# Loading the first input tile in two transfers, of 16 and of 112 partitions

## The chip, the cores and the metric

The kernel runs on one core of one Trainium2 chip. The metric is the device time of one execution in microseconds (us). The kernel before was run three times: median 630.27 us, from 630.23 to 630.30 us.

## What is computed

```python
B, S, D = 8, 2048, 4096
x: float32 [8, 2048, 4096]      # 268 MB
w: float32 [4096, 1]

proj = (x @ w).squeeze(-1)                       # one dot product of 4096 per row of x
cm = np.maximum.accumulate(proj, axis=1)         # running maximum along S
is_record = (proj >= cm).astype(np.float32)
return np.cumsum(is_record, axis=1)              # running count of records, [8, 2048]
```

Nearly all of the data is x, and each of its elements is used once.

## The kernel before, in words

The rows of x are taken in groups along S. Three groups have four rows to a partition (512 rows of S each) and a fourth has three (384 rows); within a group there is one tile for each of the eight batches. A tile therefore has 128 partitions with 64 KB each (48 KB in the fourth group), and it is 8.39 MB. What is left of S, 128 rows of each batch, is the tail: eight tiles of 16 KB to a partition, the last two of them loaded in column pieces (list `TILES`).

All loads of x are issued by the SyncE queue (SP in the profile), in the order in which they are used: first the loop over groups `g` and tiles `t` (L165 to L176), then the tail (L194 to L205). There are three large buffers (`xbuf`, chosen by `at(g, t)`), so the first three loads have no wait, and each later one waits until the work on the tile that had its buffer is done (`user_before` and `free`, on the semaphores `fr` and `p7`). Each load adds 16 to a semaphore of its tile position, `xs[t]`, and the engines that read the tile wait for `xs[t]` to reach 16. The TensorE program takes these 16 off again after each group.

The work on a tile is split by columns. VectorE multiplies and sums columns 0 to 2815 of each row in one instruction (`dot`, L124, called from `group_dots`). GpSimd multiplies the other 1280 columns (`group_products`, L276), and ScalarE sums those products (`add_up`, L130). After a group, TensorE transposes the sums into PSUM (L312), and VectorE makes the running maximum, the comparison and the running count (`group_scans`). For the first three groups each engine's program is a hardware loop (`Fori`), whose first iteration serves the first tile too.

While the first tile loads, w is brought in by a small transfer from the ScalarE queue (L178), spread over the partitions by TensorE (L224) and copied by ScalarE (L231 to L235).

The issuing loop at the place of the change reads:

```python
i = SY.dma_start(
    out=at(g, t)[:, : r * D],
    in_=x[B - 1 - t, STARTS[g] : STARTS[g] + r * P, :].rearrange("(p r) d -> p (r d)", r=r),
).then_inc(xs[t], 16)
u, n = user_before(g, t)
if n:
    i._wait_ge(*(free(u, n)))
```

## Time and profile before

| | |
|---|---|
| Median of 3 runs | 630.27 us |
| Time of the profiled execution | 631.05 us |
| Span of its instructions in the profile | 629.3 us |
| Between the two | 1.75 us |
| Bytes read from HBM | 268.45 MB |
| VectorE (DVE) busy | 407.3 us, 65% |
| GpSimd (POOL) busy | 370.7 us, 59% |
| ScalarE (ACT) busy | 181.2 us, 29% |
| TensorE (PE) busy | 29.1 us, 5% |
| Queue of the SP loads | 98.9% of what 16 DMA engines' span holds |

All times inside the profile are counted from the start of the span. A load appears twice in it: as an instruction on the SP queue, which only hands it over, and as packets that the 16 DMA engines move, whose end is the landing. A packet of a large tile is one partition's row of 64 KB.

### The profile page before, as it was taken

What the parts mean: (1) busy time and instruction counts of PE and PEld (TensorE: products, weight loads), DVE (VectorE), ACT (ScalarE), POOL (GpSimd) and SP (SyncE); (2) the same over time, 40 slices, a digit from 0 to 9 for tenths busy, and PEclk for the clock granted to TensorE, in tenths of its full rate; (3) what the DMA queues carried; (4) which work ended last, traced back from release to release, by engine and by line L of the source; (5) the groups of instructions that cost most, each with busy time, mean ns of one, the idle gap of its engine ahead of it and who ended that gap; (6) DMA issues with size and microseconds to landing.
All of it is one profiled execution on the core that took longest, in us unless ns stands there. A gap on an engine that the chain in (4) does not pass through costs nothing. (4 is left out here: it accounts for less than half of the span.)

```text
span 629.3 us, 1140 instructions
## 1 busy us (share of the span) xinstructions
PE 29.1 (5%) x96; PEld 13.5 (2%) x96; DVE 407.3 (65%) x294; ACT 181.2 (29%) x274; POOL 370.7 (59%) x149
## 2 busy tenths in 40 slices
PE   8000000000020000000001000000002000000100
PEld 3000000000010000000000000000001000000000
DVE  0755775556766567755578655676556976655897
ACT  1222332223322233222233222332223232232254
POOL 0554675456765557745577555676557666555775
PEclk9999999999999999999996555555555555555565
DMA  9999999999999999999999999999999999999996
GB/s 401 400 467 400 446 421 425 442 437 429 442 425 450 417 450 417 459 408 458 408 458 408 458 408 458 408 459 408 462 418 438 416 447 441 413 447 444 404 425 248
DMA packets 6563, 268.54 MB, mean 427 GB/s; under 512 B 760, under 2 KB 1016, under 8 KB 1568
## 3 DMA queue, kind: packets, MB, share of 16 engines
q1 hardware_dynamic: 6544, 268.50, 98.9%
q10 hardware_dynamic: 16, 0.02, 0.0%
q14 instruction: 3, 0.02, 0.0%
HBM read 268.45 MB, written 0.07 MB: 427 GB/s over the span
## 5 line engine op out<-in xcount | busy, mean ns | idle before, releaser
L124 DVE CUSTOM_DVE_ANT_0 xall<-xall,w_v 128x2816 f32<-128x2816 f32 (+1 forms) x129 | 385.5, 3041 | 181.8 <-DMA xall<-in_x_dram 181.8
L276 POOL TENSOR_TENSOR xall<-xall,w_sb 128x1280 f32<-128x1280 f32 x120 | 345.0, 2909 | 246.7 <-DMA xall<-in_x_dram 243.3
L130 ACT ACTIVATE xall<-xall 128x1280 f32<-128x1280 f32 (+2 forms) x130 | 162.9, 1253 | 428.6 <-POOL xall L276 408.3
L312 PE MATMUL ps<-identity,small 128*8 128x128 f32 x60 | 13.0, 406 | 568.6 <-PEq L309 568.6
L130 ACT ACTIVATION_READ_ACCUMULATOR xall<-xall 128x1 f32 x130 | 24.2, 186 | 0.0
L336 POOL TENSOR_TENSOR xall<-xall,w_sb 128x1280 f32<-128x1280 f32 (+2 forms) x8 | 21.1, 2632 | 3.1 <-DMA xall<-in_x_dram 3.0
L312 PEld LDWEIGHTS ps<-identity,small 128*8 128x8 f32 x60 | 7.3, 125 | 575.4 <-issue 571.3
L140 DVE TENSOR_TENSOR_SCAN cm<-ps,cm,small 8x512 f32<-8x512 f32 (+3 forms) x8 | 7.0, 869 | 18.8 <-PE ps L312 18.4
L224 PE MATMUL w_v<-w,identity 8*128 8x512 f32 x14 | 12.1, 1056 | 0.0
L124 DVE DVE_READ_ACCUMULATOR2_ANT small<- 128x1 f32 x133 | 10.8, 81 | 0.0
L246 DVE MEMSET ps<- 8x512 f32 x1 | 0.5, 485 | 15.7 <-ACT w L235 15.7
L146 DVE TENSOR_TENSOR_SCAN cnt<-ps,cnt,small 8x512 f32<-8x512 f32 (+3 forms) x8 | 7.0, 870 | 0.3
L224 PEld LDWEIGHTS w_v<-w,identity 8*128 8x128 f32 x14 | 4.6, 332 | 7.3 <-issue 7.3
L143 DVE TENSOR_TENSOR ps<-ps,cm 8x512 f32<-8x512 f32 (+3 forms) x8 | 3.9, 487 | 0.3
L232 ACT COPY w_sb<-w_v 128x768 f32<-128x768 f32 x1 | 0.8, 799 | 11.4 <-PE w_v L224 11.4
L347 POOL TENSOR_TENSOR masked<-fold,small 128x4 f32<-128x4 f32 x8 | 1.6, 201 | 3.2 <-DVE small L124 3.2
L124 DVE CUSTOM_DVE_ANT_0 xall<-xall,w_v,small 128x480 f32<-128x480 f32 (+2 forms) x4 | 3.1, 810 | 0.2 <-DVE small L124 0.2
L357 PE MATMUL ps<-fold,masked 128*8 128x32 f32 x20 | 2.0, 235 | 25.3 <-ACT masked L352 17.7
L352 ACT ACTIVATE masked<-fold,small 128x4 f32<-128x4 f32 x10 | 3.0, 298 | 0.3
L336 POOL TENSOR_TENSOR xall<-xall,w 128x640 f32<-128x640 f32 (+1 forms) x2 | 2.3, 1137 | 0.1
L224 PE MATMUL ps<-w,identity 8*128 8x512 f32 x2 | 2.1, 1135 | 2.6 <-DMA w<-in_w_dram 2.6
L231 ACT ACT_TABLE_LOAD x1 | 1.3, 1283 | 2.7 <-DVE fold L242 2.7
(18 smaller groups left out, 5.3 us busy)
## 6 DMA issues: line engine op xcount, KB each, us to landing
xall<-in_x_dram SPq DMA_DIRECT2D x8, 6144.0 KB, 33.5
xall<-in_x_dram SPq DMA_DIRECT2D x6, 2048.0 KB, 42.4
xall<-in_x_dram SPq DMA_DIRECT2D x1, 1264.0 KB, 36.6
xall<-in_x_dram SPq DMA_DIRECT2D x1, 816.0 KB, 39.3
xall<-in_x_dram SPq DMA_DIRECT2D x1, 784.0 KB, 37.9
xall<-in_x_dram SPq DMA_DIRECT2D x2, 240.0 KB, 26.6
xall<-in_x_dram SPq DMA_DIRECT2D x1, 416.0 KB, 39.4
xall<-in_x_dram SPq DMA_DIRECT2D x24, 45.0
```

What stands on the lines that cost most here:

```text
L124: return V.tensor_tensor_reduce(out=xsl, in0=xsl, in1=wsl, scale=1.0, scalar=seed, op0=ALU.mult, op1=ALU.add, accum_out=dst,)
L130: return A.activation(out=xsl, in_=xsl, func=ACTF.Copy, accum_out=dst)
L140: V.tensor_tensor_scan(out=cm_, data0=src, data1=low, initial=cm0, op0=ALU.max, op1=ALU.max,)._wait_ge(psr, base).then_inc(psr, 1)
L143: V.tensor_tensor(out=src, in0=src, in1=cm_, op=ALU.is_ge)._wait_ge(psr, base + 1).then_inc(psr, 1)
L146: V.tensor_tensor_scan(out=cnt_, data0=src, data1=low, initial=cnt0, op0=ALU.add, op1=ALU.max,)._wait_ge(psr, base + 2).then_inc(cs, 1)
L224: i = T.matmul(out=dst, lhsT=identity[:NW, k : k + 1].to_broadcast([NW, P]), rhs=w_row, start=True, stop=True,).then_inc(bw, 1)
L276: i = G.tensor_mul(out=xl, in0=xl, in1=w_sb).then_inc(pl, 1)
L312: i = T.matmul(out=ps[:B, j : r * P : r], lhsT=l[:, j * B : (j + 1) * B], rhs=identity, start=k == 0, stop=k == 1,)
L336: G.tensor_mul(out=xl, in0=xl, in1=w_pool(*p))._wait_ge(xq[i], 16).then_inc(pl, 1)
L347: return eng.tensor_tensor(out=e, in0=by_b, in1=acc.to_broadcast([P, H]), op=ALU.mult)
L352: return A.activation(out=e, in_=by_b, func=ACTF.Copy, scale=acc)._wait_ge(pa, na).then_inc(ms, 1)
L357: return T.matmul(out=ps[:B, k * Q : (k + 1) * Q], lhsT=masked[:, n * B : (n + 1) * B], rhs=by_i, start=start, stop=stop,)
```

## The change

The load of tile `g == t == 0`, and no other, is issued as two instructions: the first has partitions 0 to 15 and adds 16 to a new semaphore, `xf`; the second has partitions 16 to 127 and adds 16 to `xs[0]` as before. VectorE and GpSimd each get one wait for `xf` ahead of their loops, and the wait for `xs[0]` stays where it was.

```diff
-    ws, bw, ... mg, pg, ml = (
+    ws, bw, ... mg, pg, ml, xf = (
...
         for g in range(NG):
             r = RS[g]
             for t in range(B):
-                i = SY.dma_start(
-                    out=at(g, t)[:, : r * D],
-                    in_=x[B - 1 - t, STARTS[g] : STARTS[g] + r * P, :].rearrange(
-                        "(p r) d -> p (r d)", r=r
-                    ),
-                ).then_inc(xs[t], 16)
+                src = x[B - 1 - t, STARTS[g] : STARTS[g] + r * P, :].rearrange(
+                    "(p r) d -> p (r d)", r=r
+                )
+                p0 = 0
+                if g == t == 0:
+                    p0 = P // 8
+                    SY.dma_start(out=at(g, t)[:p0, : r * D], in_=src[:p0]).then_inc(
+                        xf, 16
+                    )
+                i = SY.dma_start(out=at(g, t)[p0:, : r * D], in_=src[p0:]).then_inc(
+                    xs[t], 16
+                )
...
+        V.wait_ge(xf, 16)
         with V.Fori(0, NL):
             group_scans()
...
+        G.wait_ge(xf, 16)
         G.wait_ge(wc, 3)
         with G.Fori(0, NL):
             group_products(R)
```

## The prediction

> **What bounds the kernel now.** I read the page first, its DMA rows, then its chain and its costliest groups, then the waits of the engines and of the SP queue, and last the timeline of the start.

> ```profile
> DMA  9999999999999999999999999999999999999996
> ...
> q1 hardware_dynamic: 6544, 268.50, 98.9%
> ...
> L124 DVE CUSTOM_DVE_ANT_0 xall<-xall,w_v 128x2816 f32<-128x2816 f32 (+1 forms) x129 | 385.5, 3041 | 181.8 <-DMA xall<-in_x_dram 181.8
> L276 POOL TENSOR_TENSOR xall<-xall,w_sb 128x1280 f32<-128x1280 f32 x120 | 345.0, 2909 | 246.7 <-DMA xall<-in_x_dram 243.3
> ```

> The DMA row stands at 9 from the first slice to the last but one: the load queue fills 98.9% of the span. The two busiest engines wait for loads and for little else (181.8 and 243.3 us). So the kernel is one stream of loads.

> ```profile
> SPq L168 <- ACT xall L130: 415.5, 20, 38.9
> SPq L168 <- DVE small L124: 65.3, 4, 19.9
> ```

> The SP queue waits for buffers, but that starves nothing: two more tiles are queued while a buffer is being used. The timeline of the start gives the pace and the price of starting:

> ```profile
> 0.91 0.60 ACTq L178 DMA_DIRECT2D w<-in_w_dram  x1
> ...
> 0.97 54.41 SPq L168 DMA_DIRECT2D xall<-in_x_dram  x5
> ...
> 2.62 2.07 PE L224 MATMUL ps<-w,identity 8*128 8x512 f32 x2 [2.62 <-DMA w<-in_w_dram]
> ...
> 22.80 3.09 DVE L124 CUSTOM_DVE_ANT_0 xall<-xall,w_v 128x2816 f32<-128x2816 f32 x1 [0.67 <-DMA xall<-in_x_dram]
> ...
> 42.08 3.09 DVE L124 CUSTOM_DVE_ANT_0 xall<-xall,w_v 128x2816 f32<-128x2816 f32 x1 [7.16 <-DMA xall<-in_x_dram]
> ```

> VectorE's first dots of tiles 0 and 1 start as their tiles land, 42.08 - 22.80 = 19.28 us apart. A tile of 8.39 MB in 19.28 us is 435 GB/s, 27.2 GB/s for each of 16 engines. An engine moves 8 of the 128 partitions, so one partition of 64 KB takes 19.28 / 8 = **2.41 us, called a slot below**. From issue to use tile 0 takes 22.80 - 0.97 = 21.83 us: 19.28 us at pace and 2.55 us of starting.

> Check: 268.45 MB at 435 GB/s are 617.1 us; with issue at 0.97 and 2.55 of starting the loads end at 620.6 by this sum. In stretches of the trace, loads still run at 322 GB/s from 622 to 623 us and are over by 624; the missing 3 us (0.5%) are stretches a little under pace. After it come only the last sums, scans and the store, issued at 626.39 us. Whatever the load stream loses at its start, the end loses.

> [...]

> **The change part by part.**

> 1. *A second issue on SP.* The SP queue needs 0.33 us for one load (median of the 32 at L168). All loads after it, and the store of the first counts, move back by 0.33 us. Cover: the first transfer lasts at least one slot, 2.41 us, and tiles 1 and 2 are not due for 20 us. Cost 0; without the cover 0.33 us.
> 2. *Smaller first transfer.* If the engines get their first packets sooner, the stream starts sooner. A bound from above: starting costs 2.55 us for x, and the small load of w needs 1.71 us from issue to use, so at most 0.8 us can go. The other bound is that w started no sooner than x, which gives 0. I take 0.2 us; from -0.8 to +0.3 with the cover of part 1 gone.
> 3. *The waits for `xf`.* VectorE's stands ahead of the first scans (L140, at 18.83 us), GpSimd's ahead of its wait for w. In the trace both engines wait until 22.8 us for tile 0 anyway, and partitions 0 to 15 start first. If the first transfer landed after 18.83 us, three scans (1.27 + 0.69 + 1.27 us) would follow it, still before the other 112 partitions. Cost 0.[...]
> 4. [...]with a quarter of the trace's pace it takes 4 slots, 9.6 us[...]. Before, the same engines had moved four partitions each in that time. [...]**the stream is at least 4 slots, 9.6 us, late.**
> 5. *Partitions 16 to 127 on 16 engines.* [...]tile 0 ends after 4 + 11 = 15 slots instead of 8: 7 late, 16.9 us. With perfect spreading it is 4 + 8 = 12: 4 late, 9.6 us. How the pieces are dealt out is not in the trace, so I take the middle, 5.5 slots = 13.3 us[...], with both ends kept for the range.
> 6. *Does it come back?* No. After tile 0 every engine has as many bytes to move as before and the pace is the same; the slowest engine, 13.3 us late, always has two tiles queued. Buffers: the dots of a tile take VectorE 12.1 us of a 19.28 us interval, so compute is not next in line.

> Sum: 13.3 - 0.2 + 0 = +13.1 us. On the profiled execution, 631.05 + 13.1 = 644.1 us (span 642.4); the median of the runs stands 0.12% below that execution, so **630.27 + 13.1 = 643.4 us**. The case's own range is +9.3 to +19.5 us[...]: 639.6 to 649.8 us.

> **The rivals.**

> - [...]The limit is the engine, 27.2 GB/s wherever it writes. Then the 16 first packets take 2.41 us each, the seven others follow without a gap, and only parts 1 and 2 are left: -0.2 us, 630.1 us, between 629.5 and 630.6. For it: [...]the last tail pieces keep 413 GB/s though their source is laid out differently.[...] It decides if a first packet keeps more than about 17 GB/s, that is takes under 3.8 us, since 1.3 us are what a measurement can tell.
> - *The transfer is not one partition per engine.* [...]the 16 go to four engines, four each, and the other twelve start with the second transfer, 0.33 us later. Every engine still moves eight: +0.3 us, 630.6 us.[...]
> - *The 112 are dealt out in turn,* partition 16 + e to engine e and so on. [...]32 slots instead of 8, +24 slots = 58 us, 688 us.[...]
> - *Faster.* The first packets start sooner by all of the 0.8 us[...]: 629.5 us, still within 0.2%. For more, something else at the start would have to shrink, and the profile shows nothing that could.

> **How the numbers follow.** A measurement of this kernel can tell about 0.2%, 1.3 us, from no change. [...]639.6 to 649.8 us: 0.66. [...]up to the dealing in turn: 0.08. [...]629.5 to 630.9 us: 0.23. Faster by over 1.3 us for a reason that I do not see: 0.03. So faster 0.03, same 0.23, slower 0.74. Predicted time 643.4 us; the range must reach to the second case, since leaving it out would lose more than 2 in 10: 629.6 to 650.0 us.

> **What would show it.** In the profile after: VectorE's first dot (22.80 us before) at 32 to 40 us if parts 4 and 5 are right, unchanged within 0.8 us[...], and near 81 us if the 112 are dealt out in turn. GB/s in the first two slices of the page (401 and 400 before) well below, and from the fifth on as before. The intervals between later tiles stay 19.28 us, and the store moves from 626.39 us by as much as the first dot did. The prediction is wrong if the first dot is late but the end is not, or if later tiles come at another pace.

## The result, and the profile after

The change made the kernel slower: 650.70 us (650.38 to 651.19, 4 runs) against 630.28 us (630.23 to 630.51, 4 runs), a ratio of 1.0324 (95% interval 1.0306 to 1.0342), or **+20.4 us**. The profiled execution after has a span of 649.4 us, 20.1 us more than the 629.3 us before. +13.1 us had been forecast.

The page of the kernel after, its rows that answer to those shown before, and the rate in 40 slices of 16.2 us:

```profile
GB/s 142 254 307 420 428 448 448 400 449 444 432 416 448 444 412 440 449 432 412 452 440 424 428 448 440 408 449 440 428 424 436 433 436 436 434 433 430 418 429 251
...
q1 hardware_dynamic: 6560, 268.50, 98.8%
...
L124 DVE CUSTOM_DVE_ANT_0 xall<-xall,w_v 128x2816 f32<-128x2816 f32 (+1 forms) x129 | 385.5, 3041 | 199.9 <-DMA xall<-in_x_dram 199.9
L283 POOL TENSOR_TENSOR xall<-xall,w_sb 128x1280 f32<-128x1280 f32 x120 | 344.9, 2909 | 266.9 <-DMA xall<-in_x_dram 263.6
```

The rate before, in slices of 15.7 us:

```profile
GB/s 401 400 467 400 446 421 425 442 437 429 442 425 450 417 450 417 459 408 458 408 458 408 458 408 458 408 459 408 462 418 438 416 447 441 413 447 444 404 425 248
```

The load queue is still "busy" for 98.8% of the span, with the same bytes. Busy is not at pace: the first three slices move 142, 254 and 307 GB/s where 401, 400 and 467 were moved before, and from the fourth on the rate is what it was. The engines' own work has not changed (385.5 and 344.9 us); their waits for loads have grown by 18.1 and 20.3 us. Those 20 us are the change.

The timeline of the same execution, at its start, at the first dots of tiles 0 and 1, and at the store of the end:

```profile
0.97 0.40 SPq L174 DMA_DIRECT2D xall<-in_x_dram  x1
...
1.43 56.89 SPq L177 DMA_DIRECT2D xall<-in_x_dram  x4
...
4.40 2.07 PE L230 MATMUL ps<-w,identity 8*128 8x512 f32 x2 [4.40 <-DMA w<-in_w_dram]
...
45.02 3.09 DVE L124 CUSTOM_DVE_ANT_0 xall<-xall,w_v 128x2816 f32<-128x2816 f32 x1 [21.11 <-DMA xall<-in_x_dram]
...
64.30 3.09 DVE L124 CUSTOM_DVE_ANT_0 xall<-xall,w_v 128x2816 f32<-128x2816 f32 x1 [7.17 <-DMA xall<-in_x_dram]
...
646.51 0.32 SPq L421 DMA_DIRECT2D out_dram<-cnt  x1
```

Before, the store stood here:

```profile
626.39 0.32 SPq L413 DMA_DIRECT2D out_dram<-cnt  x1
```

The first dot stands at 45.02 us in place of 22.80: 22.2 us late. Tile 1 follows 19.28 us behind it, the old pace. The store is 20.1 us late. So all of the loss lies in tile 0, and some 2 us of it come back later (the last experiment looks into these). The answer on line L174 alone gives the first transfer, 1 MiB, from issue to landing:

```profile
L174 SPq DMA_DIRECT2D xall<-in_x_dram x1: 400/400/400, 1.0 to 1.0; - x1
...
DMA to landing us min/median/max: 12.4/12.4/12.4
```

The records of single packets in the two traces (a packet is one partition's 64 KB; sixteen run at a time, as many as the page counts DMA engines) show where the time in tile 0 goes. A record names neither its engine nor its partition, so the packets are taken sixteen at a time in the order of their starts; the k-th sixteen is called step k of a transfer below. Medians of each sixteen, in us:

| step of tile 0 | 1 | 2 | 3 | 4 | 5 | 6 | 7 | 8 |
|---|---|---|---|---|---|---|---|---|
| before | 3.08 | 2.42 | 2.42 | 2.42 | 2.42 | 2.42 | 2.42 | 2.42 |
| after | 8.55 | 5.25 | 4.73 | 3.15 | 3.85 | 4.74 | 4.74 | 4.52 |

The first step is partitions 0 to 15: all sixteen packets are under way between 1.99 and 12.08 us, 104 GB/s for the 1 MiB. The seven other steps are the second transfer; their medians sum to 31.0 us, and before they took 16.9.

### The profile page after: what moved, and what is told of

Read it like the earlier page. It is cut to its first block, busy times and chain, and to the rows that moved or that the text cites. A ratio compares the mean times of both kernels' runs of the same rounds, so it can differ in the third digit from the quotient of the medians.

```text
span 649.4 us, 1142 instructions
## 1 busy us (share of the span) xinstructions
PE 29.4 (5%) x96; PEld 13.7 (2%) x96; DVE 407.3 (63%) x294; ACT 181.2 (28%) x274; POOL 370.6 (57%) x149
## 2 busy tenths in 40 slices
DMA  9999999999999999999999999999999999999996
## 3 DMA queue, kind: packets, MB, share of 16 engines
q1 hardware_dynamic: 6560, 268.50, 98.8%
HBM read 268.45 MB, written 0.07 MB: 413 GB/s over the span
## 5 line engine op out<-in xcount | busy, mean ns | idle before, releaser
L124 DVE CUSTOM_DVE_ANT_0 xall<-xall,w_v 128x2816 f32<-128x2816 f32 (+1 forms) x129 | 385.5, 3041 | 199.9 <-DMA xall<-in_x_dram 199.9
L283 POOL TENSOR_TENSOR xall<-xall,w_sb 128x1280 f32<-128x1280 f32 x120 | 344.9, 2909 | 266.9 <-DMA xall<-in_x_dram 263.6
L130 ACT ACTIVATE xall<-xall 128x1280 f32<-128x1280 f32 (+2 forms) x130 | 162.9, 1253 | 446.9 <-POOL xall L283 426.5
L320 PE MATMUL ps<-identity,small 128*8 128x128 f32 x60 | 13.3, 414 | 586.6 <-PEq L317 586.6
L130 ACT ACTIVATION_READ_ACCUMULATOR xall<-xall 128x1 f32 x130 | 24.2, 186 | 0.0
L140 DVE TENSOR_TENSOR_SCAN cm<-ps,cm,small 8x512 f32<-8x512 f32 (+3 forms) x8 | 6.9, 869 | 19.1 <-PE ps L320 18.7
L230 PE MATMUL w_v<-w,identity 8*128 8x512 f32 x14 | 12.1, 1056 | 0.0
L252 DVE MEMSET ps<- 8x512 f32 x1 | 0.5, 485 | 17.5 <-ACT w L241 17.5
L124 DVE DVE_READ_ACCUMULATOR2_ANT small<- 128x1 f32 x133 | 10.8, 81 | 0.0
L124 DVE CUSTOM_DVE_ANT_0 xall<-xall,w_v,small 128x480 f32<-128x480 f32 (+2 forms) x4 | 3.1, 800 | 0.2 <-DVE small L124 0.2
```

What stands on the lines that cost most here:

```text
L124: return V.tensor_tensor_reduce(out=xsl, in0=xsl, in1=wsl, scale=1.0, scalar=seed, op0=ALU.mult, op1=ALU.add, accum_out=dst,)
L130: return A.activation(out=xsl, in_=xsl, func=ACTF.Copy, accum_out=dst)
L140: V.tensor_tensor_scan(out=cm_, data0=src, data1=low, initial=cm0, op0=ALU.max, op1=ALU.max,)._wait_ge(psr, base).then_inc(psr, 1)
L230: i = T.matmul(out=dst, lhsT=identity[:NW, k : k + 1].to_broadcast([NW, P]), rhs=w_row, start=True, stop=True,).then_inc(bw, 1)
L283: i = G.tensor_mul(out=xl, in0=xl, in1=w_sb).then_inc(pl, 1)
L320: i = T.matmul(out=ps[:B, j : r * P : r], lhsT=l[:, j * B : (j + 1) * B], rhs=identity, start=k == 0, stop=k == 1,)
```

## The experiments

After the result both transfers were known to be slow: 8.55 us a packet for the 16 partitions and 3.15 to 5.25 for the 112, against 2.42 before. What was open: whether the destination or the source rows matter, whether splitting as such costs anything, and why the 112 partitions ran at about half pace. In three sessions the kernel before had medians of 630.36, 630.30 and 630.31 us. Loads that stand ahead of the kernel (the sets of probes and the doubled load) are edits of the kernel before; all other edits are of the changed kernel. The letters A, B and C name other theories in each experiment, those of the text above its result.

### Thirteen loads, one at a time

```diff
...
+        for k, (dst, srows) in enumerate(PROBES):
+            i = SY.dma_start(out=xbuf[2][dst, :], in_=rows[srows, :]).then_inc(pr[k], 16)
+            if k:
+                i._wait_ge(pr[k - 1], 16)
...
+                if g == t == 0:
+                    i._wait_ge(pr[-1], 16)
...
```

> Ahead of the kernel before stand 13 loads of 64 KB rows into the third buffer, each issued only when the one before it has landed: destination partitions and source rows are 0-127/0-127, 0-15/0-15, 0-15/every 8th row, every 8th partition/0-15, every 7th partition (16 of them)/0-15, 16-127/16-127, 16-127/0-111, 0-111/0-111, 0-31, 0-63, 64-127, 32-127, 16-63. A packet at full pace takes 2.42 us. Theory A[...]: 16 packets into partitions 0-15 take about 9.7 us each whatever the source rows; into every 8th partition[...] about 4.8; into every 7th[...] 2.4 for most and 4.8 for four; 0-31 gives 4.8 a packet, 0-63 and 64-127 too, and 16-127 is independent of its source rows. Theory B (the HBM side decides, by which rows are read together): destination 0-15 is slow only with rows 0-15, every 8th and 7th partition are as slow as 0-15 when rows 0-15 are read, and 16-127 changes with its source rows. For 16-127 both expect the 4.7 us a packet that the changed kernel shows, 33 us in all[...].

From the packet records (907.24 us in all, since these loads stand ahead of the kernel). The last column is the median of all packets of the load; where two values stand, they are the lowest and the highest of the medians of its steps.

| destination partitions | source rows | from first packet to last end, us | one packet, median us |
|---|---|---|---|
| 0-127 | 0-127 | 20.36 | 2.42 |
| 0-15 | 0-15 | 9.39 | 8.5 |
| 0-15 | every 8th | 9.49 | 8.4 |
| every 8th | 0-15 | 5.36 | 4.6 |
| every 7th, 0 to 105 | 0-15 | 4.98 | 4.5 |
| 16-127 | 16-127 | 31.27 | 3.2 to 4.7 |
| 16-127 | 0-111 | 32.82 | 3.1 to 4.8 |
| 0-111 | 0-111 | 31.60 | 3.4 to 4.8 |
| 0-31 | 0-31 | 10.64 | 5.1 |
| 0-63 | 0-63 | 20.85 | 5.1 |
| 64-127 | 64-127 | 20.64 | 5.1 |
| 32-127 | 32-127 | 30.34 | 4.4 to 5.1 |
| 16-63 | 16-63 | 24.96 | 8.3 |

The source rows hardly matter (9.39 against 9.49 us for the 16, 31.27 against 32.82 for the 112), the destination does (sixteen packets took 9.39 us into partitions 0-15, 5.36 into every 8th): theory B, by which the source rows decide, falls. But theory A, by which the destination does, missed in one row: into every 7th partition twelve packets should have taken 2.4 us, and all sixteen took 3.9 us or more. Alone, the 112 partitions take 31.27 us, and the steps of the changed kernel sum to 31.0, so the two transfers hardly disturb each other.

### The first tile split by columns

```diff
-                p0 = 0
+                c0 = 0
                 if g == t == 0:
-                    p0 = P // 8
-                    SY.dma_start(out=at(g, t)[:p0, : r * D], in_=src[:p0]).then_inc(
+                    c0 = D // 2
+                    SY.dma_start(out=at(g, t)[:, :c0], in_=src[:, :c0]).then_inc(
                         xf, 16
                     )
-                i = SY.dma_start(out=at(g, t)[p0:, : r * D], in_=src[p0:]).then_inc(
-                    xs[t], 16
-                )
+                i = SY.dma_start(
+                    out=at(g, t)[:, c0 : r * D], in_=src[:, c0:]
+                ).then_inc(xs[t], 16)
```

> The first tile is again loaded in two transfers with the two extra waits, but split by columns: both transfers have 128 partitions, the first 8 KB and the second 56 KB of each. If a second transfer, its issue or the waits for xf cost anything, or an early start gains anything, it shows here. Theory A (narrow transfers are slow[...]): 630.3 us, within 0.8 us. Theory B (any split, or the waits, cost the 20 us): about 650 us.

Measured: 630.20 us, ratio 0.9999 (0.9990 to 1.0008). Its timeline at the start:

```profile
0.97 0.40 SPq L174 DMA_DIRECT2D xall<-in_x_dram  x1
...
1.42 1.54 SPq L177 DMA_DIRECT2D xall<-in_x_dram  x3
...
22.45 3.09 DVE L124 CUSTOM_DVE_ANT_0 xall<-xall,w_v 128x2816 f32<-128x2816 f32 x1 [0.36 <-DMA xall<-in_x_dram]
```

Two transfers, a second issue and both new waits are here, and the first dot is even 0.35 us earlier than before (22.80). Splitting by columns is free; what costs is splitting by partitions. And the 0.35 us that a small first transfer gains at the first dot don't show at the end.

### The 112 first, the 16 second

```diff
-                p0 = 0
+                p1 = P
                 if g == t == 0:
-                    p0 = P // 8
-                    SY.dma_start(out=at(g, t)[:p0, : r * D], in_=src[:p0]).then_inc(
+                    p1 = P // 8
+                    SY.dma_start(out=at(g, t)[p1:, : r * D], in_=src[p1:]).then_inc(
                         xf, 16
                     )
-                i = SY.dma_start(out=at(g, t)[p0:, : r * D], in_=src[p0:]).then_inc(
+                i = SY.dma_start(out=at(g, t)[:p1, : r * D], in_=src[:p1]).then_inc(
                     xs[t], 16
                 )
```

> Partitions 16-127 are issued first and 0-15 second. Theory A (each of the two transfers is slow for its own partitions): first dot again at about 45 us and 650 us in all, within 2 us. Theory B (the 112 are slow only because the 16 engines leave the first transfer out of step[...]): the 112 alone take 17 to 27 us in place of 33, and the time is 640 to 645 us.

Measured: 651.57 us, ratio 1.0338 (1.0321 to 1.0355), and the first dot of this kernel at

```profile
45.66 3.09 DVE L124 CUSTOM_DVE_ANT_0 xall<-xall,w_v 128x2816 f32<-128x2816 f32 x1 [5.28 <-DMA xall<-in_x_dram]
```

The order hardly matters (45.66 and 45.02 us); each transfer is slow by itself, as theory A says.

### Two halves

```diff
-                    p0 = P // 8
+                    p0 = P // 2
```

> The first tile is split into partitions 0-63 and 64-127. Theory A[...]: each packet takes two slots of 2.41 us, 4 + 4 packets an engine last 16 slots in place of 8, so +19.3 us, 649.6 us; a little less if engines of the two halves overlap. Theory B (only narrow transfers or those whose count is no power of two are slow): 630.3 to 633 us.

Measured: 651.43 us, ratio 1.0336 (1.0319 to 1.0353), and the first dot at

```profile
44.51 3.09 DVE L124 CUSTOM_DVE_ANT_0 xall<-xall,w_v 128x2816 f32<-128x2816 f32 x1 [16.88 <-DMA xall<-in_x_dram]
```

In the packet records the median is 4.8 us for the first step and 4.9 to 5.1 for each of the other seven. Halves of a power of two do no better: theory B falls. A packet takes slightly more than the two slots (4.82 us) that theory A gave it, which is why it is more than +19.3.

### Fewer packets, single rows

Same edit as in the first experiment, with other sets of partitions.

> Fourteen loads of 64 KB rows stand ahead of the kernel before, one at a time: partition 0; partition 4; partition 64; eight partitions 0,4,..,28; eight partitions 4,8,..,32; eight partitions 64,68,..,92; eight partitions 0,16,..,112; partitions 0-7; sixteen partitions 0,4,..,60; 0-47; 64-111; 16-63 with every second row; 0-79; 16-127. [...] Theory A[...]: the single rows take 2.4 us into partition 0 and about 4.6 into 4 and 64; of the eights 0,4,..,28 takes 2.4 a packet, 4,8,..,32 and 64,68,..,92 about 4.6. Theory B[...]: single rows and all three of these eights take 2.4 us a packet, and only 16 engines at once are slow. Both: 0,16,..,112[...] 4.8, 0-7[...] 8.4 to 9.7 us, 0,4,..,60[...] 4.6 to 4.8. For 48 partitions, which took 8.3 us a packet from 16 to 63: if they are dealt in turn to the engines, 0-47 and 64-111 take 8.3 too, with every second row as well; if rows in HBM did it, every second row changes it. 16-127 again 31 to 33 us.

Single rows took 2.81 us (partition 0), 3.29 (4) and 3.11 (64); the eights 0,4,..,28, 4,8,..,32 and 64,68,..,92 all took 2.4 to 3.2 us a packet. 0,16,..,112 took 4.1 to 5.1, 0-7 7.9 to 8.8, and 0,4,..,60 4.4 to 5.3. So theory A, which had about 4.6 us for rows 4 and 64 and for two of these eights, falls. The 48 partitions took 8.1 to 8.3 us a packet at 0-47, 64-111 and 16-63 with every second row; 0-79 took 5.0; 16-127 again 31.90 us in all. Theory B, by which only sixteen packets at once are slow, was left; it stands as theory C in the next set, and falls there.

### Eleven sets, each loaded three times

```diff
...
+            for m in range(NS):
+                i = SY.dma_start(out=xbuf[m][dst, :], in_=rows[srows, :]).then_inc(
+                    pr[k], 16
+                )
+                if k and not m:
+                    i._wait_ge(pr[k - 1], 16 * NS)
...
```

> Eleven sets of partitions are loaded ahead of the kernel before, each three times in a row (into the three buffers) before the next set starts; 64 KB rows. [...] Theory A[...]: A, B and H run at about 2.42 us a packet after the first, and all engines of C, D, E, F, G, I at 3.2 to 4.8[...]. Theory B[...]: in C, D, F and I two engines take 4.8 and the others 2.42, in E and G four take 4.8. Theory C[...]: A and B take 4.2 to 4.7 us a packet too. All: J 4.7, K 8.5.

Three packets of a set follow one another, one from each load. The second of them, where the start no longer shows:

| set | destination partitions | packets in one load | second packet, us |
|---|---|---|---|
| A | 32,36,..,88 | 15 | 2.42 (with B: two of the 30 up to 2.65) |
| B | 18,25,..,116 | 15 | as A |
| H | 0,4,..,28 | 8 | 2.42 |
| C | 18,25,..,123 | 16 | two at 4.82, the others 2.42 to 2.62 |
| D | 3,10,..,108 | 16 | as C |
| F | 28,32,..,88 | 16 | two at 5.12, the others as in C |
| I | 0,5,..,35 | 8 | two at 4.82, the others as in C |
| E | 0,7,..,105 | 16 | 4.93 **for all sixteen** |
| G | 24,28,..,84 | 16 | 5.12 **for all sixteen** |
| J | every 8th, 0 to 120 | 16 | 5.12 for all |
| K | 0-15 | 16 | 9.64 for all |

The steps of the 112 are not slow alike. The load by itself had medians of 4.63, 4.65, **3.54, 3.22**, 4.31, 4.58 and 4.54 us. In the changed kernel, too, just two of the sixteen are slow in its third and fourth steps (4.77 and 4.78, then 4.40 and 4.80 us), as in C, D and F; but the other fourteen take 3.0 to 4.0 us, not the 2.42 of C and D. For 0-111 the fast steps were 4 and 5 (3.4 and 3.7 us). For 16-127 from source rows 0-111 only step 3 was fast (3.1 us), and step 4 took 4.2. Why these steps was not shown, since no record names an engine or a partition.

### Split at 96

```diff
-                    p0 = P // 8
+                    p0 = P // 4 * 3
```

> The first tile is split into partitions 0-95 and 96-127, six and two to an engine. Theory A[...]: [...]16 slots in place of 8, +19.3 to +20.6 us (the probes had 10.6 us for 32 partitions and 30.3 for 96), 649.6 to 650.9 us. Theory B[...]: 14 to 15 slots, +14.5 to +16.9 us, 644.8 to 647.2 us.

Measured: 650.28 us, ratio 1.0317 (1.0299 to 1.0334), in theory A's range and above B's. All packets of all eight steps take 4.3 to 5.1 us.

### A whole load ahead, and a second profile of before

The first of these asks for the 2 us that came back; its edit is the probe loop with one entry, partitions 0-127. The second is the kernel before, unchanged.

> One whole 128-partition load (20.4 us in the probes) goes ahead and lands before the first tile is issued, so all loads start about 22.2 us later at full pace. The changed kernel's first dot was 22.2 us late and its end only 20.1 us, and the kernel before has rows slower than 2.42 us between 34 and 118 us that it lacks. Theory A (a late stream escapes that slow stretch, whatever made it late): the end is 1.5 to 2.5 us less late than the first dot, about 650.5 us. Theory B (it needs the narrow transfers, or is chance of the profiled run): the end is as late as the first dot, about 652.5 us.

> The kernel before, for a second profile. If the slow rows between 34 and 118 us belong to the kernel, they come again, with about 1.1 us of excess an engine; if to one execution, they are absent or elsewhere. Time 630.3 us.

The doubled load took 652.33 us, ratio 1.0346 (1.0329 to 1.0363), +22.0 us, with the first dot at

```profile
44.83 3.09 DVE L124 CUSTOM_DVE_ANT_0 xall<-xall,w_v 128x2816 f32<-128x2816 f32 x1 [22.66 <-DMA xall<-in_x_dram]
```

that is 22.0 us late: nothing comes back, theory B. The second profile of before (630.10 us) has its first dot at 22.89 and its store at 625.44 us, 602.55 us apart, against 603.59 in the first profile: one microsecond of the two belonged to that execution. So the stretches from first dot to store can be compared over all the runs. Rows of 64 KB slower than 2.425 us are counted after the first step of tile 1:

| first tile loaded | first dot to store, us | slow rows |
|---|---|---|
| whole (two profiles of before) | 603.59, 602.55 | 210, 162 |
| split by columns | 602.84 | 176 |
| whole, after another whole load | 602.68 | 240 |
| 16 and 112 partitions (the change) | 601.49 | 2 |
| 112 and 16 | 601.63 | 2 |
| 96 and 32 | 602.20 | 2 |
| halves | 602.30 | 2 |

In the two profiles of before the slow rows make 1.1 and 0.3 us of excess over 2.42 us when it is shared out over 16 engines. So after every cut by partitions the slow rows are all but gone, and the rest of the kernel is 0.25 to 1.1 us faster than the fastest of the others, one profile each. Why is open: in the kernel after the starts of a step stay up to 1.66 us apart, but in the two halves they are within 0.40 us until about 126 us, and the slow rows are gone there too.

## Why the prediction was wrong in its size

- **What bounds the kernel**: right. Everything lost in tile 0 reached the end but for 1 to 2 us, and compute did not become the bound.
- **Part 1, the second issue**: right; the column split has it and stands at 0.9999.
- **Part 2, the smaller first transfer**: -0.2 us taken, no gain found. After the change the first packets start between 1.99 and 3.37 us, where they started between 1.98 and 2.60. The load of w came later too, four of its eight packets starting only between 3.15 and 3.29 us: TensorE starts at 4.40 in place of 2.62 us, hidden under tile 0.
- **Part 3, the waits**: right; VectorE's first scan moved from 18.83 to 20.61 us because of w (its wait before is put down to ScalarE's copy, 17.5 us), and the transfer of the 16 was done by then.
- **Part 4, partitions 0 to 15**: right in size. 9.6 us forecast; 7.1 to 8.8 us a packet, 10.1 us in all. The quarter of the pace, and that all 4 slots are lost, were the author's assumptions, which the trace before did not show. The rate measured here is 104 GB/s; the load alone, in the first set of probes, had 112, against 412 for the one of 128 partitions.
- **Part 5, the 112**: **the step that failed.** It set 11 slots and 8 as the ends for the 112 and took the middle. Both ends were the author's assumptions, which the trace before did not show. Measured, the 112 take 31.3 to 32.8 us, about 13.3 slots, beyond both. In sets E and G, too, the slow pace took in all sixteen packets (4.93 and 5.12 us), where theory B there had four. With 13.3 slots in the prediction's own sum, 4 + 13.3 - 8 = 9.3 slots of 2.41 us are 22.4 us, and the first dot was 22.2 us late, at 45.02 us and beyond the 32 to 40 us that had been named for it. The case's upper end (8 slots late) lay below it, and the middle, 5.5, was taken where no trace chose between its ends.
- **Part 6, does it come back**: nearly right; forecast none, measured 1.1 us against the second profile of before and 2.1 against the first.
- **The rivals**: the first, "27.2 GB/s wherever it writes", and the second, "not one partition per engine", fall with the first sixteen packets, which run at one time and take 8.55 us, over the 3.8 that was set as the deciding point; "faster" needed the first of them, too. "Dealt out in turn" falls with the 31 us of the 112: it asked for 32 - 4 = 28 slots, 68 us, and seven steps at the measured 8.55 us of partitions 0 to 15 would be 60 us, an estimate.

## What to carry to other kernels

Where loads set the time, split a tile along its free dimension and keep all 128 partitions in every transfer: two transfers by columns cost nothing here (630.20 against 630.36 us), and any cut by partitions that was tried cost 20 to 21 us on one 8.39 MB tile, half of the pace for as long as it lasted. Price a narrow transfer by a measured load into the same partitions, since their number alone does not give it: with rows of 64 KB, 16 partitions took 9.39 us in a row and 5.36 as every 8th, 48 in a row (16-63) 24.96, 64 in a row 20.6 to 20.9, the 112 31.3 to 32.8, and all 128 took 20.36. A queue that is busy for 98.8% of the span tells nothing of its rate: read the GB/s slices beside it.

## What the runs showed of the hardware that had not been expected

- In a load of sixteen 64 KB packets it can be two that are slow (4.82 us against 2.42, sets C and D) or all (4.93 and 5.12 us, sets E and G). One more partition, 28, put into the fifteen of set A slowed two packets (F, 5.12 us); 24 and 28 in place of 88 slowed all sixteen (G, 5.12 us). What couples them was not tried.
- The number of packets under way does not set their pace: sixteen into partitions 0 to 15 ran at one time and took 8.55 us each (9.64 in set K), and fifteen into the partitions of set A or B 2.42 us each. Which engine wrote where is not in the records.
- 48 partitions (0-47, 64-111, 16-63) take 8.1 to 8.3 us a packet, more than 0-31 and 0-63 (5.1 us) and not far from the 9.64 us of set K.
